# A fused two-model kernel: the last modulation steps moved behind the first direction of a recurrence in TensorE's order

## The chip, the cores and the metric

One Trainium2 chip, one of its cores. The metric is the device time of one execution in microseconds (us), lower is better. Engines: PE (TensorE), DVE (VectorE), ACT (ScalarE), POOL (GpSimd), SP (SyncE, which here only issues DMAs).

## What is computed

Two transformer blocks of two layers each run one after the other on 256 tokens of width 1024. The change lies in the last layer, whose mixer has a recurrence over the tokens (in two directions) beside a neighbourhood attention:

```python
def wkv7_step(S, inp):
    r, w, k, v, a, b = inp
    sa = jnp.einsum('bhvk,bhk->bhv', S, a)
    S = S * w[:, :, None, :] + sa[..., None] * b[:, :, None, :] + v[..., None] * k[:, :, None, :]
    return S, jnp.einsum('bhvk,bhk->bhv', S, r)
...
        mod = jnp.einsum('bd,de->be', jax.nn.silu(c), ada_w[i]) + ada_b[i]
        mod_c = jax.nn.silu(c_ctx) @ ada_w[i] + ada_b[i]
        sh1, sc1, g1, sh2, sc2, g2 = jnp.split(mod[:, None, :], 6, -1)
...
    x = x + g1 * y
    h = rms_norm_2(x, norm2_g[i]) * (1.0 + sc2) + sh2
    x = x + g2 * expert_choice_ffn(h, moe_router[i], moe_w1[i], moe_w3[i], moe_w2[i])
```

Each layer is modulated by six vectors (`sh1` to `g2`), a product of a 1024 vector with a 1024 x 6144 matrix. Behind the mixer stands a layer of 16 experts, whose weights are 192 MB.

## The kernel before, in words

All operations are written in program order, and a scheduler with a simulated timeline sets the order on each engine; within an engine the order is then fixed, and each engine and each DMA queue works through its own in that order. `later(offset, tag)` (line 300) adds to the priority number, so that a block with a large offset is put where the scheduler thinks that nothing earlier is ready.

*The recurrence* (`rwkv`, line 1897) is computed in chunks of 64 tokens. For each direction d and each of 4 blocks b of 128 channels: `decays` (1930) multiplies a triangular matrix `tri` with the gates on PE, in two halves of a block, each into a `py` bank of PSUM, takes exponentials on ACT (`win`, `AR`, `iin`, `Kh`) and forms the factors `Bh` and `Kh` on DVE and POOL. `within` (1983) forms products of these inside each chunk ("grams": `pg<-AR,Bh` on PE, masked by DVE into `Lx` and `Lc`). `spill` (1990) does the same with `Kh` (`MN`), multiplies with `V` (`py<-V,MN`), copies the result (`MV`, ACT) and transposes `Bh` and `Kh` on PE (`py<-cst,Bh`, `py<-cst,Kh`), which ACT copies (`zt`) and SP writes to DRAM (`sp<-MV`, `sp<-zt`). There are two `py` banks and two pairs of `pg` banks. With direction 0 the gates of direction 1 are prepared too (`begin(1)`, `low_rank`, line 1852).

Then each direction has a set of triangular systems: `gather` (2033) sends `Lx` and `Lc` through DRAM (`scr`) into another layout, `substitute` (2049) solves all systems of the direction at once by 31 steps of two DVE operations (`fs`, then `fsx` for direction 0 and `sgs` for direction 1), copies the result once and writes it to DRAM twice; `complete` (2067) reads it back (`kk`, `fsx`; `k`, `sgs`) and finishes the inverses on PE (`pg<-fsx,Lx` and so on; `pg<-sgs,Lx` is the first matmul of direction 1). DVE does the 62 operations of a direction between its work for `decays(1, b)`, `within(1, b)` and `spill(1, b)`. After that the chunks follow each other (the chain that begins with `pg<-mv,kk`), with the neighbourhood attention (`natten`, `pS<-nk,nq`, `pd<-low,nv`) between.

*The modulation* of this layer (`m`, `mods_steps`, line 508) is 3 banks of 8 steps; the first bank is done before the recurrence. A step is one slice of 128 rows: four loads of 128 x 512 (256 KB each, SP, `mod_weights`, 586) into the five `mw` tiles, and four matmuls, each into another 32 partitions of one `pd` bank. After the last step of a bank ACT copies it (`modrow`), PE transposes it (`pS<-cst,modrow`), DVE adds a bias (`modcol`), and the gates are transposed and written to DRAM (`gate_rows`, 545: `gatec`, `pS<-cst,gatec`, `modra`). `fill(n)` (2099) adds n steps at priority offset `OLATE`; `need(m, 2)` adds whatever is left. The `mw` tiles share their slots (tag `n2`) with the attention's `nbias` tiles.

Of the kernel before, what the change touches and what calls it, by code (L numbers as in the profile page):

```python
# [253 lines left out]
class Kernel:  # L254
# [75 lines left out]

    def mm(self, out, lhsT, rhs, start, stop):
        ins = self.nc.tensor.matmul(out, lhsT, rhs, start=start, stop=stop, skip_group_check=True)  # L332
        if self.pin:
            self.tc.keep_in_program_order(ins)
        return ins
# [1334 lines left out]

T2 = 16
SUB0, SUB1 = 0, 0
OLATE, OF = 2000, (2, 2, 2)
DECAY = math.exp(-0.5)


# [18 lines left out]
class Odd(Moe):  # L1695
# [201 lines left out]
    def rwkv(self, od, core, m):  # L1897
        nc, tc, a = self.nc, self.tc, self.a
# [15 lines left out]
        def begin(d):  # L1914
            S = st[d]

            S["AR"] = core.tile([128, 4, 768], F32, name=f"AR{d}")
            S["ARx"] = S["AR"][:, :, :512].rearrange("p b (i k t) -> p b i k t", k=4, t=64)
            S["sp"] = self.dram.tile([4, 128, 3, 512], F32, name=f"sp{d}")
            S["WC"] = core.tile([128, 4, 8], F32, name=f"WC{d}")  # L1920
            S["gr"] = core.tile([128, 2, 4, 2, 128], F32, name=f"Lx{d}")
            S["sgs"], S["av"] = self.rates[0] if d == 0 else self.low_rank(1, core, "t2", T2, "py")
# [60 lines left out]
        def within(d, b):  # L1983

            for th in range(2):
                p, mask = gram(st[d][b][0], d, b, th)
                L = st[d]["Lc"][:, :, b] if th else st[d]["gr"][:, :, b]
                nc.vector.tensor_tensor(L.rearrange("p t h c -> p h t c"), p, mask, OP.mult)
# [44 lines left out]
        def gather(d):  # L2033

            Lx, Lc = st[d]["gr"], st[d]["Lc"]
            scr = [self.dram.tile([4, 32, 32, 32], F32, name=f"scr{d}{i}") for i in range(3)]
            for q in range(4):
                hf, b2 = q // 2, q % 2
                ps_ = slice(64 * hf + 32 * b2, 64 * hf + 32 * b2 + 32)
                cs = slice(32 * b2, 32 * b2 + 32)  # L2040
                for i, gr in ((0, Lx[..., 64 * hf:64 * hf + 64]), (1, Lc)):
                    src = gr[ps_].rearrange("p t b h c -> p (t b h) c")[:, :, cs]
                    nc.sync.dma_start(scr[0][q, 16 * i:16 * i + 16].rearrange("u s t -> s u t"), src)
            LM = od.tile([128, 2, 32, 32], F32, name="sgs", bufs=1) if d else st[0]["LX"]
            LM, X = LM[:, 0], LM[:, 1]
            nc.sync.dma_start(LM, scr[0].rearrange("q u s t -> (q u) s t"))
            st[d].update(scr=scr, LM=LM, X=X)
# [51 lines left out]
        def fill(n):  # L2099
            with self.later(OLATE, "pS"):  # L2100
                self.fill(n)
# [3 lines left out]
        for b in range(4):  # L2105
            if b < 3:
                decays(0, b + 1)
            if b == 2:
                begin(1)
            within(0, b)  # L2110
            spill(0, b)
            fill(OF[0])
        gather(0)
        with self.later(SUB0, "pS"):
            substitute(0)
        for b in range(4):
            decays(1, b)
            within(1, b)
            fill(OF[1])
        gather(1)  # L2120
        with self.later(SUB1, "pS"):
            substitute(1)
        for b in range(4):
            spill(1, b)
            fill(OF[2])
        with self.later(OLATE, "pS"):
            self.need(m, 2)

        td = [p.tile([128, 4, 4, 2, 64], F32, name=n, bufs=1) for p, n in ((od, "kk"), (od, "k"))]
# [187 lines left out]
```

## Time and profile before

| | |
|---|---|
| median of 3 runs | 2812.18 us (2805.17 to 2812.28) |
| the profiled execution | 2812.01 us, span 2810.2 us |
| PE busy in the span | 2549.2 us (91%) |
| DVE, ACT, POOL busy | 1222.0, 773.3, 306.9 us |
| DMA | 683.94 MB, mean 243 GB/s |
| mean granted clock of PE | 0.957 |

The busy shares are averages over stages with different limits, so a stage is read by itself: its stretch of the span, who is busy in it, and which wait ends last. The granted clock is a share of full speed (2.4 GHz); PE has two levels, 1.2 and 2.4 GHz, and a share between stands for a stretch with both. In the trace a full-precision matmul has two rows. All times below are microseconds from the start of the span.

### The profile page before, as it was taken

To read this page: it belongs to the slowest core of one execution; us is meant where nothing else is said; L and a number is where in the kernel's file an instruction comes from. 1 tells how busy PE (TensorE), PEld (TensorE's weight loads), DVE (VectorE), ACT (ScalarE), POOL (GpSimd) and SP (SyncE) were. 2 spreads that over 40 slices of the span, in tenths; PEclk is the share of its full clock that TensorE was granted. 3 is DMA by queue.
4 is the path that set the end of the run, shared out by engine and by line. 5 is a ranking of instruction groups with operands and counts; after the bars stand their busy time and mean duration, and the time that the engine had idled before them with its cause. 6 is when DMAs were issued, how large, how long until landed. Compare 5 with 4: busy or idle time off the path is not lost.

```text
span 2810.2 us, 34392 instructions
## 1 busy us (share of the span) xinstructions
PE 2549.2 (91%) x13731; PEld 1567.7 (56%) x13731; DVE 1222.0 (43%) x2337; ACT 773.3 (28%) x1395; POOL 306.9 (11%) x372
## 2 busy tenths in 40 slices
PE   7999899996988998989899999989996997888888
PEld 4667688885866796757633333348644684222221
DVE  3355633448767467997511111145449452000000
ACT  3342322222333344276510000033442432000000
POOL 0001400004102003300100000000033130000000
PEclk9999999998989999999999999999998898999999
DMA  7443522233546854242699999963185548999998
GB/s 314 150 165 120 210 105 92 104 120 107 211 144 263 297 184 171 70 169 76 255 403 422 421 421 421 421 238 104 47 239 137 150 157 353 414 427 427 427 427 353
DMA packets 147360, 683.94 MB, mean 243 GB/s; under 512 B 38400, under 2 KB 51584, under 8 KB 72064
## 3 DMA queue, kind: packets, MB, share of 16 engines
q1 hardware_dynamic: 140656, 663.91, 61.2%
q10 hardware_dynamic: 6544, 17.83, 2.0%
q8 instruction: 108, 1.77, 0.3%
q14 instruction: 52, 0.43, 0.0%
HBM read 668.25 MB, written 11.60 MB: 242 GB/s over the span
## 4 chain that ended last, share of the span: by engine, by line
PE 52%; DMA 25%; DVE 8%; ACT 2%; issue 2%; POOL 1%; SPq 0%; ACTq 0%; DVEq 0%; POOLq 0%
DMA w<-in_moe_w 22%; PE pd L332 18%; PE pS L332 12%; PE pu L332 6%; PE pt L332 5%; PE ps L332 3%; PE pg L332 2%; PE pm L332 1%; DVE al L369 1%; PE pt L477 1%; PE ps L477 1%; DMA w<-in_od_w_in 1%; PE pO L332 1%; DVE fs L2060 1%; DVE co L1194 1%
## 5 line engine op out<-in xcount | busy, mean ns | idle before, releaser
L332 PE MATMUL pu<-w,xs 128*64 128x512 f32 (+1 forms) x2040 | 493.4, 599 | 40.9 <-DMA w<-in_moe_w 40.9
L352 ACT CAST wh<-w 128x1024 fp32r<-128x1024 f32 x250 | 259.5, 1041 | 602.9 <-PE pd L332 280.2
L355 DVE TENSOR_TENSOR wl<-w,wh 128x1024 fp32r<-128x1024 f32 x229 | 286.1, 1252 | 316.8 <-ACT wh L352 316.1
L332 PEld LDWEIGHTS pu<-w,xs 128*64 128x64 f32 (+1 forms) x2040 | 149.9, 123 | 367.1 <-issue 256.2
L332 PE MATMUL pd<-w,hidT 128*64 128x512 f32 (+1 forms) x1024 | 253.2, 598 | 28.8 <-DMA w<-in_moe_w 28.1
L332 PE MATMUL pd<-ah,wh 128*128 128x512 f32 (+2 forms) x656 | 232.9, 360 | 7.7 <-ACT wh L352 3.5
L332 PE MATMUL pd<-al,wh 128*128 128x512 f32 (+2 forms) x656 | 231.0, 354 | 7.5 <-DVE al L369 7.5
L332 PE MATMUL pd<-ah,wl 128*128 128x512 f32 (+1 forms) x648 | 226.3, 351 | 0.0
L1648 DVE TENSOR_TENSOR hid<-hid,pu 128x512 f32<-128x512 f32 x24 | 16.5, 688 | 434.4 <-PE pu L332 434.4
L1647 ACT ACTIVATE hid<-pu 128x512 f32<-128x512 f32 x24 | 14.2, 597 | 673.0 <-PE pu L332 673.0
L332 PEld LDWEIGHTS pd<-w,hidT 128*64 128x64 f32 (+1 forms) x1024 | 75.2, 123 | 197.3 <-issue 115.5
L332 PEld LDWEIGHTS pd<-ah,wh 128*128 128x128 f32 (+1 forms) x656 | 127.1, 195 | 40.2 <-issue 14.4
L332 PEld LDWEIGHTS pd<-al,wh 128*128 128x128 f32 (+1 forms) x656 | 128.0, 195 | 26.4 <-DVE al L369 8.9
L1657 DVE TENSOR_TENSOR ys<-pd,g 128x512 f32<-128x512 f32 x24 | 16.6, 692 | 282.4 <-PE pd L332 282.4
L332 PEld LDWEIGHTS pd<-ah,wl 128*128 128x128 f32 x648 | 126.2, 195 | 21.7 <-issue 7.5
L332 PE MATMUL pm<-w,sil 128*32 128x512 f32 x512 | 87.4, 711 | 30.8 <-DMA w<-in_ada_w 15.1
L1667 DVE TENSOR_TENSOR X<-X,ps 128x512 f32<-128x512 f32 x80 | 54.8, 688 | 109.2 <-PE ps L332 109.2
L1194 DVE SCALAR_TENSOR_TENSOR co<-cv,cols,co 128x512 f32<-128x512 f32 x120 | 100.6, 863 | 0.4
L332 PE MATMUL pS<-al,wh 128*128 128x256 f32 (+1 forms) x264 | 90.2, 342 | 5.5 <-DVE al L369 5.5
L332 PE MATMUL pS<-ah,wh 128*128 128x256 f32 (+1 forms) x264 | 90.1, 342 | 1.3 <-ACT ah L368 1.3
L332 PE MATMUL pS<-ah,wl 128*128 128x256 f32 (+1 forms) x264 | 89.3, 338 | 0.0
L354 POOL CAST hh<-tf 128x512 fp32r<-128x512 f32 (+1 forms) x64 | 37.3, 583 | 432.9 <-DVE tf L987 421.5
(601 smaller groups left out, 4527.2 us busy)
## 6 DMA issues: line engine op xcount, KB each, us to landing
w<-in_moe_w SPq DMA_DIRECT2D x383, 1024.0 KB, 19.6
w<-in_w_mod SPq DMA_DIRECT2D x32, 1024.0 KB, 6.0
w<-in_w_up SPq DMA_DIRECT2D x32, 1024.0 KB, 4.8
w<-in_w_down SPq DMA_DIRECT2D x32, 1024.0 KB, 4.8
w<-in_ada_w SPq DMA_DIRECT2D x32, 1024.0 KB, 5.0
w<-in_w_in SPq DMA_DIRECT2D x20, 1024.0 KB, 4.9
w<-in_modT SPq DMA_DIRECT2D x16, 1024.0 KB, 4.9
mw<-in_ada_w SPq DMA_DIRECT2D x64, 256.0 KB, 3.7
```

The source lines that it names most:

```text
L332: ins = self.nc.tensor.matmul(out, lhsT, rhs, start=start, stop=stop, skip_group_check=True)
L352: nc.scalar.copy(h, src)
L354: he.tensor_copy(h, src)
L355: (le or nc.vector).tensor_tensor(l, src, h.bitcast(F32), OP.subtract)
L369: nc.vector.tensor_tensor(l, t, h.bitcast(F32), OP.subtract)
L477: ins = self.nc.tensor.transpose(out, in_, self.ident[:rows, :rows])
L1194: nc.vector.scalar_tensor_tensor(y, CV[:, f, :, t:t + T], self.col(f"dw{t}", f), y, OP.mult, OP.add)
L1647: nc.scalar.activation(hid[:, cs], up["moe_w1_2"][c], AF.Silu)
L1648: nc.vector.tensor_tensor(hid[:, cs], hid[:, cs], up["moe_w3_2"][c], OP.mult)
L1657: nc.vector.tensor_tensor(ys[:, cs], down[c], gate[:, cs], OP.mult)
L1667: nc.vector.tensor_tensor(self.X[tb][:, cs], self.X[tb][:, cs], ps, OP.add)
L2060: nc.vector.tensor_tensor(t, LM[:, s, tr, None].to_broadcast([128, nt_, nj]), X[:, s, None, jr].to_broadcast([128, nt_, nj]), OP.mult)
```

## The change

Each matmul now leaves its instruction in `self.pe`. The fills behind `spill(0, b)` are gone. `held` is the last matmul of `spill(0, 3)`, and the modulation steps' PE instructions get an edge that puts them behind it in PE's order: two steps behind each `within(1, b)` and two behind each `spill(1, b)`. The edge is on PE alone; the loads on SP have none.

```diff
     def mm(self, out, lhsT, rhs, start, stop):
         ins = self.nc.tensor.matmul(out, lhsT, rhs, start=start, stop=stop, skip_group_check=True)
+        self.pe = ins
...
-OLATE, OF = 2000, (2, 2, 2)
+OLATE = 2000
...
             within(0, b)
             spill(0, b)
-            fill(OF[0])
+        held = self.pe
         gather(0)
         with self.later(SUB0, "pS"):
             substitute(0)
         for b in range(4):
             decays(1, b)
             within(1, b)
-            fill(OF[1])
+            with tc.issue_after(held.ins):
+                fill(2)
         gather(1)
         with self.later(SUB1, "pS"):
             substitute(1)
         for b in range(4):
             spill(1, b)
-            fill(OF[2])
-        with self.later(OLATE, "pS"):
+            with tc.issue_after(held.ins):
+                fill(2)
+        with self.later(OLATE, "pS"), tc.issue_after(held.ins):
             self.need(m, 2)
```

PE before, in the middle of the first direction (`pd<-mw,sil` are modulation matmuls):

```order
L332 MATMUL py<-V,MN 64x64 x16
L332 MATMUL pd<-mw,sil 32x512 x2
L332 MATMUL py<-V,MN 64x64 x8
L477 MATMUL py<-cst,Bh 128x128 x4
L332 MATMUL pd<-mw,sil 32x512
L332 MATMUL pg<-AR_13886,Bh 64x128 x8
L332 MATMUL pg<-AR_13886,Bh 64x64 x5
L477 MATMUL py<-cst,Kh 128x128 x4
```

The changed kernel has none there; 46 of the 64 stood in this direction before, the first now stands behind its last `py<-V,MN`.

PE of the changed kernel at the end of the second direction, from the last spilled block to the completion:

```order
L478 MATMUL py<-cst,Kh 128x128 x4
L332 MATMUL py<-V,MN 64x64 x24
L478 MATMUL py<-cst,Bh 128x128 x4
L332 MATMUL pd<-mw,sil 32x512
L478 MATMUL py<-cst,Kh 128x128 x4
L332 MATMUL pd<-mw,sil 32x512 x18
L478 MATMUL pS<-cst,modrow 128x128 x4
L478 MATMUL pS<-cst,gatec 16x128
L332 MATMUL pg<-fsx,Lx_13889 64x32 x32
```

Before, `pg<-fsx,Lx` followed the last `py<-cst,Kh` at once.

SP's queue of the changed kernel from the writing of the second direction's systems (`scr<-sgs`) to the attention's `nbias`:

```order
L592 DMA mw<-in_ada_w 128x512 x5
L2065 DMA scr_14874<-sgs 128x1024
L592 DMA mw<-in_ada_w 128x512
L2066 DMA scr_14875<-sgs 128x1024
L592 DMA mw<-in_ada_w 128x512 x4
L2080 DMA k<-scr_14875 32x32x32 x4
L2080 DMA sgs<-scr_14874 32x32x32 x4
L592 DMA mw<-in_ada_w 128x512 x3
L1884 DMA nbias<-in_na_bias 128x512 x4
```

Before, the two writes, the eight reads and three `nbias` loads followed each other with no `mw` load between. Ahead of this piece the changed queue has the four `sp<-zt` of the last block, and further up one run of 23 `mw` loads ahead of the second direction's gather.

## Rows read from the trace of the kernel before

**Rows 1.** Chain that ended last, a piece late in the span: start, us, what.
```profile
2443.60 19.57 DMA w<-in_moe_w
```
**Rows 2.** Timeline of SP's queue, its first expert loads: start, us, engine, line, operation.
```profile
2300.44 29.55 SPq L1628 DMA_DIRECT2D w<-in_moe_w  x15
```
**Rows 3.** Busy by stretch: PE, PEld, DVE, ACT, POOL (count); clock, DMA share, GB/s.
```profile
2033.90:2099.40 65.50, 64.17 (x591) 27.13 (x593) 30.04 (x51) 28.08 (x67) 20.48 (x22) 0.96 0.74 216
2099.40:2180.40 81.00, 52.60 (x744) 34.23 (x739) 75.33 (x181) 24.45 (x65) 28.36 (x24) 0.85 0.57 156
...
2180.40:2224.00 43.60, 37.27 (x466) 27.63 (x462) 17.42 (x37) 16.72 (x35) 1.80 (x1) 0.69 0.45 116
```
**Rows 4.** The same of the tile mw alone: PE, PEld, clock, DMA share, GB/s.
```profile
2033.90:2099.40 65.50, 32.95 (x92) 4.41 (x92) 0.96 0.74 216
2056.10:2067.60 11.50, 6.33 (x13) 0.83 (x12) 1.00 0.81 240
2099.40:2130.00 30.60, 12.94 (x36) 1.73 (x36) 0.94 0.65 201
```
**Rows 5.** Waits from 2033.9 to 2099.4: us in total, times, longest.
```profile
DVE Lx L1988 <- PE pg L332: 7.9, 3, 4.1
...
DVE Lc L1988 <- PE pg L332: 7.1, 3, 4.0
...
DVE MN L2001 <- PE pg L332: 5.1, 3, 2.9
```
**Rows 6.** Timeline of PE, ACT and DVE, one block of the first direction.
```profile
2056.12 0.38 PE L332 MATMUL py<-tri,sgs 128*128 128x256 f32 x1
...
2056.90 0.38 ACT L1947 ACTIVATE win<-py 128x256 f32<-128x256 f32 x1 [3.24 <-PE py L332]
...
2057.76 0.84 ACT L1959 ACTIVATE Kh<-av,ik,cols 128x512 f32<-128x512 f32 x1
...
2061.34 0.68 DVE L1958 TENSOR_TENSOR Bh<-Bh,iin 128x512 f32<-128x512 f32 x1
...
2063.84 0.68 PE L332 MATMUL py<-V,MN 64*64 64x64 f32 x16
...
2064.45 0.66 PE L477 MATMUL py<-cst,Bh 128*128 128x128 f32 x4
...
2067.66 0.39 PE L332 MATMUL py<-tri,sgs 128*128 128x256 f32 x1
```
**Rows 7.** The tile mw, its loads.
```profile
DMA to landing us min/median/max: 2.7/3.7/5.9
```
**Rows 8.** Timeline of PE, from the last spilled block to the chunk chain.
```profile
2173.70 1.06 PE L477 MATMUL py<-cst,Kh 128*128 128x128 f32 x4
...
2179.90 2.06 PE L332 MATMUL pg<-fsx,Lc 64*64 64x32 f32 x64
...
2193.42 3.62 PE L332 MATMUL pg<-sgs,Lx 64*64 64x32 f32 x62 [1.18 <-DMA sgs<-scr]
...
2224.06 0.97 PE L332 MATMUL pg<-mv,kk 64*64 64x64 f32 x13
```
**Rows 9.** Timeline of SP's queue, its issues.
```profile
2069.86 15.17 SPq L591 DMA_DIRECT2D mw<-in_ada_w  x13
...
2105.39 19.52 SPq L591 DMA_DIRECT2D mw<-in_ada_w  x13
...
2174.61 3.44 SPq L2031 DMA_DIRECT2D sp<-zt  x4
...
2180.39 0.34 SPq L2065 DMA_DIRECT2D scr<-sgs  x1
...
2187.50 3.52 SPq L2079 DMA_DIRECT2D sgs<-scr  x4
```
**Rows 10.** Timeline of ACT and PE behind a bank's last modulation matmul.
```profile
2129.72 0.58 ACT L531 COPY modrow<-pd 128x512 f32<-128x512 f32 x1 [6.74 <-PE pd L332]
...
2132.13 0.27 PE L477 MATMUL pS<-cst,gatec 128*16 128x128 f32 x1 [0.28 <-DVE gatec L551]
```

## The prediction

> **What bounds the kernel now.** I read the chain that ended last, then busy time by stretch, then the waits, then the timelines of PE and of SP's queue around the recurrence. The end of the kernel is a stream of expert weights: the chain hangs on one load after another [rows 1]. SP issues the first of those loads at 2300.44 us, after its last work for the recurrence [rows 2], and nothing behind it has slack. So what the recurrence gains or loses up to there is passed on microsecond for microsecond.
>
> The recurrence has three parts here. **First direction** (2033.9 to 2099.4, 65.5 us): PE is busy 64.17 us, DVE 30.04, ACT 28.08 [rows 3]; PE bounds it. Of PE's 64.17 us the modulation matmuls take 32.95 [rows 4]. **Triangular systems** (2099.4 to 2180.4, 81.0 us): DVE is busy 75.33, PE 52.60 [rows 3], of which 12.94 are modulation [rows 4]; DVE bounds it. **Completion and first attention heads** (2180.4 to 2224.0): PE 37.27 of 43.6 us at a granted clock of 0.69 [rows 3].
>
> **The change, part by part.** No operation is added or removed. There are 64 modulation matmuls (the trace has two rows for each), 46 in the first part and 18 in the second; each has its own load of 256 KB into one of five tiles. By the order none is left in the first part, 46 stand between the second part's matmuls, and 18 in one run behind the last of these, with the transposes that read them, ahead of the completion. The loads on SP's queue move along, but for the first five. Their small ACT, DVE and ACT-queue operations I cost at nothing until the last transposes: ACT is busy 24.45 of 81.0 us, and one bank's DVE work falls behind the systems.
>
> *First part: 17 us gained.* The bounds: nothing, if other engines were as late as PE; at most the time that DVE waited for PE here, 7.9 + 7.1 + 5.1 = 20.1 us [rows 5], since DVE's path starts the triangular system. Between them I walk one block in the new order, from its first `tri` half to the next block's; before, that took 2067.66 - 2056.12 = 11.54 us [rows 6]. Without modulation: a `tri` half until ACT reads it 0.8; win, AR and iin 0.9, Kh 0.8, the second half's three 0.9 (ACT); two multiplications and a mask at 0.6 (DVE); the V,MN group 0.6, the transposes of Bh and of Kh 0.6 each (PE); grams and hand-overs 1.2, my estimate. That is 8.2 us, with ACT and the two `py` banks late now instead of PE. The modulation taken out of the block is 6.33 us [rows 4]; 3.3 of them are gained, 0.53 of each microsecond. Of 32.95 us that is 17.4. I take 17: the part then lasts 48.5 us.
>
> *Second part: 2 us lost.* PE has 81.0 - 52.6 = 28.4 us free and gets some 11 us more modulation here (46 matmuls in about 24 groups of 1 us, 12.94 away). DVE's work is the same. But loads come at the pace of five tiles: 13 in a row took SP 15.17 and 19.52 us [rows 9], 1.2 to 1.5 us each, at 3.7 us to landing [rows 7]. 46 of them fit into 81 us, yet some grams of the second direction now stand behind a matmul that waits for its load, and DVE, in order, waits for the grams. Between 2 us less (the last bank's DVE work goes behind) and 7 more (a rival below) I take 2.
>
> *Behind it: 18 us lost.* Let u be the end of the last Kh transposes on PE, 2173.70 + 1.06 = 2174.8 before. There the completion began; it had both systems at 2193.42, u + 18.7, and the chunk chain began at 2224.06, u + 49.3 [rows 8]. Now 18 matmuls stand between. Four have their tiles. The fifth's load is issued at u; the next five loads stand on SP behind four issues of zt, which took 3.44 us [rows 9], so they are issued from u + 3 and used by u + 10. The five after those need these tiles, and stand around the writing of the second system, from 2180.39 (u + 5.6) on: used by u + 14. The last three stand behind the reading back of that system, whose issues ended at 2187.50 + 3.52 = 2191.0 [rows 9], u + 16.2, and end 2 us later with a load ahead of the second write: issue at u + 18.5, last matmul at u + 24. Row copy, transposes, DVE and gate transposes took from 2129.72 to 2132.40 [rows 10], so the completion starts at u + 27. From its start to the chunk chain it took 49.3 us with a wait for the second system; that is there now, and PE's own work is left, about 43 us at the clock it had, about 36 at the full one (the same 62 to 64 matmuls take 2.06 us fast and 3.62 slow [rows 8]). I take 40. The chunk chain starts at u + 67 against u + 49.3. The bounds are 8 us (the run over at u + 16, the rest fast) and 28 (all of the rest slow).
>
> Weighed against the rows: once it had waited for the second system, PE ran the completion slowly although it never idled, and the whole stretch was granted 0.69 [rows 3, 8], between the two levels of 1.2 and 2.4 GHz. My 40 us lean on that stretch. The Trainium skill (TensorE: Matmul & The Clock Gate, "HAM oscillation — how this bites in real kernels") says that short bursts of matmuls between waits for DMA keep falling back to the low clock; the run of 18 is such a stretch, and by that rule the sum would be that of the second rival.
>
> *Sum:* -17 + 2 + 18 = +3 us, against the profiled execution's 2812.0 us (span 2810.2), which lies 0.2 below the median of the runs: 2815 us. Three large terms nearly cancel; a measurement of this kernel can tell about 0.3%, 8.4 us, from no change.
>
> **The rivals.**
> *Faster: the run of 18 is short.* If its loads come as fast as tiles come free, it is over at u + 16 and the chunk chain starts 8 us late; if the first part gives up all 20.1 us, the sum is -20 + 0 + 8 = -12: 2800 us. For it: the DMA engines have room, a share of 0.45 behind 2180.4 [rows 3]. Against it: the queue order, with three loads behind the reading back.
> *Slower: the clock.* Packed with modulation the first part was granted 0.96; with 52.6 of 81.0 us busy the second was granted 0.85 [rows 3]. If PE, now with gaps, has 1.2 GHz for half of the first part, its shares of the walk grow and the gain is 12; if the completion is slow throughout, it takes 50 us instead of 40. Sum: -12 + 2 + 28 = +18: 2830 us. It decides from a granted clock below 0.8 in both stretches. The skill's rule named above is this rival.
> *Slower: DVE starved in the second part.* In one run SP's queue has the 23 loads that precede the second direction's gather. At 1.5 us each instead of 1.2 they end 7 us later, the second system starts late, and the sum is -17 + 2 + 7 + 18 = +10: 2822 us. Against it: DVE has the rest of the first system to do meanwhile.
> That the change does nothing can be left out: the order shows it.
>
> **How the numbers follow.** The forecast has 0.45; the faster rival 0.25; the clock 0.18; the starved DVE 0.12. Faster by over 0.3% is the first rival: 0.25. Slower is the two others: 0.30. Within: 0.45. The range goes from just below the faster rival to just above the clock's, 2798 to 2832; the forecast's own is 2806 to 2820, by the bounds nearest to each term.
>
> **What would show it.** First part: the first system starts near 2082 us instead of 2099.4, with no `mw` on PE and PE busy some 31 us. Second: from there to the last copy of the second system still 81 to 85 us. Behind: the completion's first matmul some 21 us after that copy, a run of `mw` ahead of it that waits for loads, then 40 us to the chunk chain. I am wrong if the first part gains under 12 us, if the run of 18 is over before the second system is read back, or if the second part grows by more than 6.

## The result and the profile after

The changed kernel took 2832.05 us (median of three runs, 2830.91 to 2834.74) against 2812.18: 19.9 us slower, ratio 1.0073 with an interval of 1.0051 to 1.0095. The forecast was 2815 us and no change. Its profiled execution took 2830.91 us, with a span of 2829.1.

Busy time by stretch in the changed kernel (columns as in [rows 3]): the first direction; from the first system to the end of the second; from the end of the last Kh transposes to the completion; from there to the chunk chain.

```profile
2033.10:2088.80 55.70, 41.39 (x472) 27.20 (x472) 27.46 (x46) 26.62 (x65) 20.79 (x22) 0.68 0.25 58
2088.80:2172.40 83.60, 63.84 (x673) 30.42 (x673) 75.04 (x179) 24.28 (x64) 27.84 (x24) 0.92 0.80 232
2167.20:2199.80 32.60, 20.02 (x43) 3.54 (x43) 5.33 (x20) 1.17 (x2) 1.80 (x1) 0.76 0.86 250
2199.80:2243.80 44.00, 44.00 (x609) 32.66 (x608) 17.63 (x37) 17.84 (x37) 0.00 (x0) 0.71 0.22 65
```

The first direction is 9.8 us shorter, but its clock fell from 0.96 to 0.68. The third stretch did not exist before; 18.59 of its 20.02 us on PE are modulation, against none at all in the first stretch. Its inside, in PE's timeline (start, us; in brackets the idle time before and what ended it):

```profile
2167.10 1.04 PE L332 MATMUL pd<-mw,sil 128*32 128x512 f32 x2
2168.54 2.34 PE L332 MATMUL pd<-mw,sil 128*32 128x512 f32 x6 [0.40 <-DMA mw<-in_ada_w]
2173.53 1.46 PE L332 MATMUL pd<-mw,sil 128*32 128x512 f32 x2 [2.65 <-DMA mw<-in_ada_w]
...
2192.83 4.20 PE L332 MATMUL pd<-mw,sil 128*32 128x512 f32 x6 [5.54 <-DMA mw<-in_ada_w]
2197.70 1.11 PE L478 MATMUL pS<-cst,modrow 128*128 128x128 f32 x4 [0.67 <-ACT modrow L532]
2199.49 0.37 PE L478 MATMUL pS<-cst,gatec 128*16 128x128 f32 x1 [0.67 <-DVE gatec L552]
2199.79 3.63 PE L332 MATMUL pg<-fsx,Lx 64*64 64x32 f32 x64
```

And on SP's queue, where before the reads were followed by `nbias`: the second write of the second system, its reading back, the last three loads, and the first expert load, which came at 2300.44 before [rows 2]:

```profile
2178.44 0.38 SPq L2066 DMA_DIRECT2D scr<-sgs  x1
...
2186.65 2.81 SPq L2080 DMA_DIRECT2D sgs<-scr  x4
2189.56 1.82 SPq L592 DMA_DIRECT2D mw<-in_ada_w  x3
...
2320.71 13.80 SPq L1629 DMA_DIRECT2D w<-in_moe_w  x7
```

The last three matmuls wait 5.54 us for loads issued behind the reading back of the second system. The expert stream starts 20.3 us later, and the span is 18.9 us longer: the difference arises ahead of that stream.

Stages in two profiles of each kernel, in us (starts and ends from PE's and DVE's timelines, rounded; u is the end of the last Kh transposes, as in the prediction):

| stage | before | again | after | again |
|---|---|---|---|---|
| first `tri` matmul to first system | 65.5 | 65.5 | 55.7 | 55.5 |
| to the end of the last Kh transposes (u) | 75.4 | 75.6 | 78.3 | 80.8 |
| u to the completion | 0 | 0 | 32.6 | 31.2 |
| completion to the chunk chain | 49.3 | 49.3 | 44.0 | 43.4 |
| sum | 190.2 | 190.4 | 210.7 | 210.8 |

### The profile page after: what moved, and what is told of

Its sections match the earlier page's. It is cut to its first block, busy times and chain, and to the rows that moved or that the text cites. A ratio compares the mean times of both kernels' runs of the same rounds, so it can differ in the third digit from the quotient of the medians.

```text
span 2829.1 us, 34407 instructions
## 1 busy us (share of the span) xinstructions
PE 2564.8 (91%) x13731; PEld 1572.6 (56%) x13731; DVE 1218.5 (43%) x2337; ACT 773.2 (27%) x1395; POOL 304.9 (11%) x372
## 4 chain that ended last, share of the span: by engine, by line
PE 51%; DMA 26%; DVE 7%; ACT 2%; issue 2%; POOL 1%; SPq 1%; ACTq 0%; DVEq 0%; POOLq 0%
DMA w<-in_moe_w 23%; PE pd L332 18%; PE pS L332 12%; PE pu L332 6%; PE pt L332 5%; PE ps L332 3%; PE pg L332 3%; PE pm L332 1%; DVE al L370 1%; PE pt L478 1%; DMA mw<-in_ada_w 1%; PE ps L478 1%; DMA w<-in_od_w_in 1%; PE pO L332 1%; PE py L332 1%
## 5 line engine op out<-in xcount | busy, mean ns | idle before, releaser
L332 PE MATMUL pm<-w,sil 128*32 128x512 f32 x512 | 87.1, 715 | 29.0 <-DMA w<-in_w_mod 14.1
L1668 DVE TENSOR_TENSOR X<-X,ps 128x512 f32<-128x512 f32 x80 | 54.8, 687 | 113.3 <-PE ps L332 113.3
L332 PE MATMUL ps<-ys,gt 128*128 128x512 f32 x160 | 82.7, 627 | 2.1 <-DVE X L1668 2.1
```

What stands on the lines that cost most here:

```text
L1668: nc.vector.tensor_tensor(self.X[tb][:, cs], self.X[tb][:, cs], ps, OP.add)
```

## The experiments

Unless told otherwise, edits are made to the changed kernel. "Chain" is the start of the chunk chain, counted from the first `tri` matmul: 190.2 before, 210.7 after. Ratios are to the kernel before, run beside each of them.

**Second profiles** (no edit).

> The changed kernel once more, for a second profile. If the tail's term is the run and its loads: the run from the last Kh transposes to the completion again 28 to 34 us, first part 55 to 57 us, time 2826 to 2836 us. If the first profile was an unlucky one (the completion's clock differs from profile to profile of one kernel, as the kernel with the masks first showed: 32.6 and 43.7 us): run below 26 us or completion below 36 us, time below 2824 us.

> The kernel before once more, for a second profile: the stages of the first one hold if the first part is 65 to 66 us, the second 80 to 83, and the chunk chain comes 187 to 194 us behind the first tri matmul.

The changed kernel took 2832.21 us, ratio 1.0092 (1.0075 to 1.0109); the kernel before took 2815.83 us in its one run. In the table above each stage came again within 2.5 us, so the terms belong to the kernels and not to one execution.

**Nearly no modulation**, in the changed order (e_none) and in the order before (e_noneb):

```
-            for k in range(KT):
+            kn = 1 if self.modpool else KT
+            for k in range(kn):
...
-                            k == 0, k == KT - 1)
-                if k < KT - 1:
+                            k == 0, k == kn - 1)
+                if k < kn - 1:
```

> The changed kernel with one step instead of eight in each of the two modulation banks of the recurrence: 14 of 16 steps, 56 of the 64 loads and matmuls, are left out. What stays is the order of the change with nothing to hide and next to nothing in the run at the end. Clock theory (PE without modulation falls to 1.2 GHz in the first part, and the run at the end is the tail's cost): first part again 54 to 57 us, clock again below 0.75; the last Kh transposes within 3 us of the changed kernel; from there to the chunk chain 43 to 50 us instead of 76.6; time 2832 - 30 = about 2802 us. Rival (the first part was slowed by the loads and tiles of the modulation, which the change only moved): first part 48 to 50 us and time 2794 us. Rival (the tail is slow for the clock alone, run or no run): from the last transposes to the chunk chain 60 us or more, 2818 us.

> The kernel before the change with one step instead of eight in each of the two modulation banks (56 of 64 loads and matmuls left out), in its own order: the 8 that stay are in the first part. It shows what the modulation cost before the change, the most that any hiding can give back. If the first part's floor is 55.7 us whatever the order (clock and low-rank chain): first part 55 to 59 us, and the time is 2802 to 2808 us, as with the changed order. If the changed order has a disadvantage of its own: 2797 us or less.

Changed order: 2805.17 us, ratio 0.9985 (0.9972 to 0.9997), chain 185.3. First part and tail came as expected (55.7 us; u to the chain 44.7), but u came 84.9 us after the first system instead of 78.3, 6.5 us later, outside the expected 3. Order before: 2814.01 us, ratio 1.0012 (0.9995 to 1.0029), chain 192.2, slower than expected. First directions of e_none and of e_noneb, and the completion of e_noneb:

```profile
2034.90:2090.60 55.70, 41.46 (x472) 27.27 (x472) 27.44 (x46) 26.62 (x65) 20.77 (x22) 0.68 0.24 57
```
```profile
2034.00:2088.80 54.80, 45.32 (x498) 26.70 (x498) 29.50 (x55) 28.22 (x69) 20.52 (x22) 0.78 0.31 80
...
2172.20:2226.20 54.00, 54.00 (x610) 38.99 (x609) 17.80 (x37) 18.52 (x37) 1.32 (x1) 0.56 0.36 88
```

So about 55 us is what the first direction takes with next to no modulation, in either order; the loads that the change moved have no part in it. And taking 56 of 64 matmuls out of the kernel before saves nothing that can be measured: what the first direction gains (10.7 us) goes into a second part 83.4 us long up to u (75.4 before) and a completion at a clock of 0.56, 54.0 us instead of 49.3. Why u comes later in both, these runs leave open. Before the change the modulation was as good as free; there was little to win.

**The tail alone** (e_tail): 12 of 16 steps free to go into the first direction, four held ahead of the completion.

```
             spill(0, b)
-        held = self.pe
+            fill(2)
...
-            with tc.issue_after(held.ins):
-                fill(2)
+            if b < 2:
+                fill(2)
...
             spill(1, b)
-            with tc.issue_after(held.ins):
-                fill(2)
+        held = self.pe
```

> The tail alone: 12 of the 16 steps may go into the first direction as before the change (the order puts 48 matmuls there), and only the last 16 matmuls are held behind the second direction's last spilled block, ahead of the completion. Theory (the run costs what its loads take, and the first part's gain is another matter): first part 64 to 67 us as before at a clock above 0.9, from the last Kh transposes to the chunk chain 20 to 27 us more than the 49.3 before, time 2812 + 20 to 27 = 2832 to 2839 us. Only 5 + 11 matmuls wait there and the tiles are free early, so the lower end is likelier. Rival (the tail cost came from the moved first part, which makes loads stand late everywhere): under 10 us more, time below 2822 us.

2826.66 us, ratio 1.0068 (1.0041 to 1.0095). First part 65.0 at a clock of 0.96; u to the completion 17.5, u to the chain 59.4, chain 204.3. The tail costs 10 us more than before, not 20 to 27, and u itself comes 4.5 us later (79.8 us after the first system, 75.4 before). The run of 16 is about half as long as that of 18 in the changed kernel; its last five loads were issued at u + 6.6, ahead of the reading back, where the changed kernel's last three came at u + 22.4, behind it. The direction was right, the size was not; the rival's 10 us were missed by little, its time by 5 us.

**A fourth back in the first direction** (e_mid1).

```
             spill(0, b)
-        held = self.pe
+            held = self.pe
+            fill(1)
```

> A fourth of the modulation back in the first direction: one step behind each of its four blocks (16 matmuls there by the order), the 48 others held as in the change and all but 5 of them between the second part's matmuls. Theory (clock and run): the first part is granted more than 0.8 and takes 54 to 58 us, no longer than without any modulation; the run at the end is gone, from the last Kh transposes to the chunk chain 45 to 52 us; time 2800 to 2808 us. Rival (PE's work sets the first part): it grows by 16 x 0.72 = 11.5 us to 67 us and all of the change's gain is gone, 2812 to 2816 us. Rival (the loads, not the order, set the end): the run is gone but the last loads still come late, the tail stays above 65 us, 2825 us.

2823.19 us, ratio 1.0056 (1.0040 to 1.0073): a miss. First part (58.1 us, at a clock of 0.79) and run (3.2) came close to what was expected, but the second part grew to 93.7 us and the completion had a clock of 0.58. SP's queue shows a part of the cause, the run of loads ahead of the second gather (25.44 us for the same 23 in the changed kernel):

```profile
2110.76 31.54 SPq L592 DMA_DIRECT2D mw<-in_ada_w  x23
2142.34 0.42 SPq L2044 DMA_DIRECT2D scr<-Lx  x1
```

The gather starts 46.7 us after the first system instead of 42.2, and later DVE waits 4.1 us (0.9 in the changed kernel) before the column add of a bank (`modcol`), whose transposes are late on PE. This looks like my rival of the starved DVE, in another kernel than the one it was written for; no run took these waits away to test it.

**Idle matmuls for the clock**: 16 in the blocks (e_warm), or 4 in the low-rank part (e_warmL).

```
+        idle = self.psum("pd")
+
+        def warm(n, pe):
+            with self.later(OLATE, "pS"), tc.issue_after(pe.ins):
+                for _ in range(n):
+                    nc.tensor.matmul(idle[:32], self.ident[:, :32], self.tri, start=True, stop=True, skip_group_check=True)
+
+        warm(4, self.pe)
...
-        held = self.pe
+            held = self.pe
+            if b < 3:
+                warm(4, held)
```

(This is e_warm; e_warmL has the same loop without `later`, called with 2 from `low_rank` in its first two steps of direction 1.)

> The changed kernel with 16 idle matmuls of the modulation's shape in the first part, on tiles that lie in SBUF, into the bank that is free there: 4 ahead of the first block and 4 behind each of the first three. They compute nothing that is used and load nothing. Clock theory: the first part is granted more than 0.85, its low-rank matmuls take 2.1 us for two instead of 3.78, and though PE has some 11 us more to do the part gets shorter, 50 to 54 us instead of 55.7; time 2826 to 2830 us. Rival (the first part hangs on ACT and DVE, not on PE's clock): it stays at 55 to 57 us whatever the clock. Rival (PE's work sets it): 60 us or more, 2837 us.

> The changed kernel with 4 idle matmuls of the modulation's shape, nothing computed with them and nothing loaded: two behind each of the first two low-rank matmuls of the second direction, where the changed kernel's PE waits 0.4 and 1.6 us before it goes on at 1.2 GHz. Clock theory: the six low-rank matmuls behind them stay at 1.0 to 1.1 us for two records instead of 1.9, the stretch from the first low-rank matmul to the mask of the last block (17.5 us in the changed kernel) takes 12 to 14 us, and the first part 51 to 53 us instead of 55.7. Rival (ACT and DVE set this stretch): clock high, but the first part still 55 us or more. Rival (the clock falls there anyway): granted clock below 0.7 from the low-rank matmuls on, first part 56 to 58 us.

e_warm: 2846.51 us, ratio 1.0149 (1.0130 to 1.0169). Its first part, halved at the first low-rank matmul, and the same of the changed kernel:

```profile
2036.80:2070.40 33.60, 28.47 (x354) 18.02 (x353) 18.21 (x31) 14.79 (x46) 15.15 (x16) 0.85 0.21 55
2070.40:2091.80 21.40, 19.41 (x145) 9.24 (x144) 9.00 (x16) 10.37 (x18) 5.08 (x7) 0.84 0.30 65
```
```profile
2033.10:2061.40 28.30, 21.35 (x337) 17.45 (x337) 17.07 (x29) 14.24 (x43) 14.67 (x15) 0.74 0.18 48
2061.40:2088.80 27.40, 20.03 (x137) 9.76 (x136) 10.39 (x18) 12.39 (x23) 6.11 (x8) 0.62 0.32 68
```

The low-rank half is 6.0 us shorter at 0.84, the other 5.3 longer by the idle work: 55.0 us in all. How much of the 6.0 is the clock, and how much ACT and DVE catching up in the longer half, this run cannot say. e_warmL (2834.01 us, ratio 1.0093, 1.0071 to 1.0115): the low-rank matmuls next to the idle ones stayed fast (1.12 us for two records), the clock fell on the four behind them after two waits of 1.4 and 1.5 us, and the first part took 57.6 us. In neither did idle work on PE make the first part clearly shorter. In both, the second part was longer too, 89.5 and 90.9 us; why, these runs leave open.

**The run cut short** (e_short), the rest as in e_none:

```
-            for k in range(KT):
+            kn = 4 if self.modpool and bank == 2 else KT
+            for k in range(kn):
```

> The changed kernel with four of the eight steps of the last modulation bank left out (16 of 64 loads and matmuls; that bank's result is then a sum over half of its rows): the order leaves 3 or 4 matmuls behind the second part instead of 18. Theory (the run is the tail's cost): first part 55 to 57 us as in the changed kernel, from the last Kh transposes to the chunk chain 46 to 54 us instead of 76.6, time 2804 to 2811 us. Rival (the 46 matmuls among the second part's own starve DVE and only the shift of the bottleneck hid it): the second part grows to 88 us or more and the time stays above 2818 us.

2809.12 us, ratio 1.0001 (0.9987 to 1.0015). First part 55.7, u to the completion 3.9, u to the chain 53.4: with the run the tail's cost goes, and the chain (190.0) is where it was before the change. The rival had a point too: the second part took 90.2 us, with a wait of DVE that stands between the steps of the second system:

```profile
DVE modcol L541 <- PE pS L478: 4.6, 1, 4.6
```

**Loads of the last five steps on ACT's queue** (e_queue).

```
...
-                self.nc.sync.dma_start(wt, src[:, g * 512:(g + 1) * 512])
+                eng.dma_start(wt, src[:, g * 512:(g + 1) * 512])
...
```

(`eng` is `nc.scalar` for `bank == 2 and k > 2`, else `nc.sync`.)

> The changed kernel with the loads of the last five modulation steps (20 of 64 loads) issued from ACT's queue instead of SP's, where three of them stood behind the reading back of the second system. PE's order keeps a run of 17. If the queue's order sets the length of the run (my step for the tail): the longest wait of the run, 5.5 us, goes, the run from the last Kh transposes to the completion takes 20 to 24 us instead of 32.6, and the time is 2820 to 2824 us. Rival (the DMA engines set it: their share was 0.86 in the run): it stays at 28 us or more, 2828 to 2834 us. Rival (ACT, held up by issues that wait for tiles, copies late): the second system ends later by 5 us or more, 2836 us.

2818.95 us, ratio 1.0046 (1.0023 to 1.0068). The run: 22.1 us, its longest wait 2.5; u to the chain 54.7 instead of 76.7. The second system ended 91.0 us after the first began (83.6 in the changed kernel), so ACT's issues seem to have cost something. The DMA engines did not set the length of the run: their share was 1.02 in it, against 0.86, and it was shorter. But these 22 us are not all the queue's. Of them 11.4 are the completion, which had the full clock in this profile (32.6 us instead of 44.0). The run gives the other 10.6, and u itself came 6.0 us later, so from the first system the completion began only 4.6 us earlier (106.4 us instead of 111.0).

**The first system behind the last mask** (e_mn, and again as e_mn2).

```
-                nc.vector.tensor_tensor(MN, p, mask, OP.mult)
+                self.mn = nc.vector.tensor_tensor(MN, p, mask, OP.mult)
...
         gather(0)
-        with self.later(SUB0, "pS"):
+        with self.later(SUB0, "pS"), tc.issue_after(self.mn.ins):
             substitute(0)
```

> The changed kernel with the first direction's triangular system ordered behind that direction's last mask on DVE. In the changed kernel the last mask stood behind eight steps of the system, so the last spilled block, and with it the first modulation matmul that is held behind it, came at 2096 us, 7.5 us after the system had begun. Theory (the whole stream of loads starts with it and ends as much earlier): first modulation matmul 3 us or less after the system's first step, the run at the end shorter by 5 to 9 us (23 to 27 instead of 32.6), time 2823 to 2827 us. Rival (PE order and tiles set it, not the start): run unchanged within 2 us, 2830 to 2833 us.

> The same kernel as the one with only the first direction's system behind the last mask on DVE, once more. In its first profile the chunk chain stood 185.5 us behind the first tri matmul, 4.6 less than before the change, and the first expert load at 2299.5 us; but the expert loads then moved 387 and 400 GB/s for 200 us where all other profiles show 427, and the time was 2821.5 us. If that was a disturbance of that run: 427 GB/s there, time 2803 to 2815 us. If the kernel causes it: again below 405 GB/s, 2819 us or more.

2821.51 us, ratio 1.0042 (1.0022 to 1.0062), then 2817.30, 1.0016 (0.9998 to 1.0034). The first modulation matmul came before the system's first step (2089.83 against 2093.42; in the changed kernel it came 7.5 us after that step), the first part stayed at 55.8 us, and the run took 26.3 and 27.2 us, as the theory had it. From the first system the completion began 97.1 and 97.9 us later, instead of 111.0. The two profiles differ in the completion, and with it in the chain (185.5 and 197.4):

```profile
2190.50:2223.20 32.70, 32.70 (x610) 24.41 (x609) 17.50 (x37) 17.53 (x37) 0.00 (x0) 1.00 0.45 121
```
```profile
2189.70:2233.40 43.70, 43.40 (x610) 31.82 (x609) 17.62 (x37) 17.95 (x37) 0.00 (x0) 0.73 0.35 92
```

The same 610 records take 32.7 us at the full clock and 43.7 at 0.73. The question put to e_mn2 has a mixed answer: the expert loads were fast again (420 and 427 GB/s), but the time stayed above the 2803 to 2815 us that were expected for that.

**Idle matmuls in the gap of the run** (e_gap), behind its 15th matmul:

```
+                    if self.modpool and bank == 2 and k == 7 and g == 1:
+                        idle, ins = self.psum("py"), self.pe
+                        for _ in range(6):
+                            with self.tc.issue_after(ins.ins):
+                                ins = nc.tensor.matmul(idle[:32], sl[:, k, :], self.V[:, 0], start=True, stop=True,
+                                                       skip_group_check=True)
...
```

> The changed kernel with 6 idle matmuls of the modulation's shape on tiles that lie in SBUF, between the 15th and the 16th matmul of the run at the end, where PE waited 5.5 us for the last three loads. Loads, their order and everything else are as in the change. Clock theory (that wait takes PE to 1.2 GHz and the completion pays for it): the wait in the run is under 2 us, the completion is granted 0.9 or more and takes 33 to 37 us to the chunk chain instead of 44.0, the run is no longer than 34 us, time 2820 to 2826 us. Rival (the completion is slow by itself, by its small matmuls and the waits for ACT and DVE): granted 0.7 as before, 43 to 45 us, time 2831 to 2835 us.

2828.50 us, ratio 1.0055 (1.0035 to 1.0075): the theory fell. The 5.5 us wait was filled and the completion began fast, but not for long:

```profile
2189.12 5.31 PE L531 MATMUL py<-V,sil 128*32 128x512 f32 x12
2195.27 2.40 PE L332 MATMUL pd<-mw,sil 128*32 128x512 f32 x6 [0.84 <-DMA mw<-in_ada_w]
2198.35 0.66 PE L478 MATMUL pS<-cst,modrow 128*128 128x128 f32 x4 [0.68 <-ACT modrow L543]
2199.67 0.27 PE L478 MATMUL pS<-cst,gatec 128*16 128x128 f32 x1 [0.67 <-DVE gatec L563]
2199.87 2.06 PE L332 MATMUL pg<-fsx,Lx 64*64 64x32 f32 x64
2201.86 3.50 PE L332 MATMUL pS<-nk,nq 64*128 64x512 f32 x4
```

The first group took 2.06 us instead of 3.63, then the clock fell after all, and the completion took 47.9 us at 0.64. In the 25 us ahead of it PE had not waited longer than 0.89 us at a time, so a long wait just ahead of the completion is not needed for a slow one. What made the clock fall here, the run does not show.

**Two attempts at a better kernel**, both with e_mn's edit: two steps back in the first direction (e_half, the diff), or the second bank's loads on ACT's queue (e_best2, as e_queue but for all `k`).

```
             spill(0, b)
-        held = self.pe
+            held = self.pe
+            if b < 2:
+                fill(1)
```

> Two changes to the changed kernel: the first direction's system is ordered behind that direction's last mask on DVE, and one modulation step stands unheld behind each of the first two blocks of the first direction (8 matmuls there by the order); 5 matmuls are left in the run at the end. Theory (first part at its floor, run short, completion at full clock): first part 55 to 58 us, second part 82 to 86, chunk chain 176 to 184 us behind the first tri matmul where the kernel before took 190.2 and the changed one 210.7: time 2798 to 2808 us. Rival (the floor that the kernel without most modulation showed, 2805, is all there is, and each load that PE waits for in the second part delays DVE): 2808 to 2818 us.

> The changed kernel with the first direction's system behind the last mask on DVE and all loads of the second of the two modulation banks (32 of 64) issued from ACT's queue; a run of 8 matmuls is left at the end. Theory: first part 56 us, run 10 to 16 us, completion 33 us, chunk chain 178 to 186 us behind the first tri matmul, time 2800 to 2810 us. Rival (ACT's issues wait for tiles and hold its copies, so that DVE waits in the second part): second part 90 us or more, time 2815 to 2825 us.

2819.19 us, ratio 1.0024 (1.0010 to 1.0037), and 2816.81, 1.0018 (0.9996 to 1.0041): both theories missed. In e_half the first part took 53.9 us, but the second 93.7, and the completion 54.0 at a clock of 0.56 (chain 202.3); in e_best2 the run took 13.7, but the second system ended only 86.7 us after the first began and the completion took 44.6 at 0.71 (chain 197.1). Neither beats the kernel before.

## Why the prediction was wrong

The chain came 20.5 us later instead of 3: 9.8 gained in the first direction, 2.9 lost up to u, 27.4 lost behind it. Two terms were mis-sized, the gain by 7 us and the tail by 9; the prediction's own sign of being wrong, a gain under 12 us, came true.

**First direction: forecast 17 us gained, measured 9.8.** The step that failed is "Of 32.95 us that is 17.4", one block's ratio spread over the whole part. The walk itself was good: the block took 8.8 us from `tri` to `tri` (2050.66 to 2059.44), 8.2 were forecast. The tile `mw` in the kernel before, halved at the first low-rank matmul (columns as in [rows 4]):

```profile
2033.90:2072.10 38.20, 19.71 (x54) 2.58 (x54) 0.94 0.69 206
2072.10:2099.40 27.30, 13.24 (x38) 1.83 (x38) 1.00 0.81 230
```

Ahead of the low-rank matmuls the part went from 38.2 to 28.3 us, with 19.71 us of modulation gone: half of each microsecond, as in the block. From the low-rank matmuls on it went from 27.3 to 27.4, with 13.24 gone: nothing. There PE's own work grew from 14.1 us (27.3 less 13.24, at full clock) to 20.0 at 0.62 (the halves beside e_warm's), and the rest became waits for ACT, DVE and the gather. The runs with next to no modulation put the whole part at 54.8 and 55.7 us, far above the forecast's 48.5.

How much of this the clock did can be read closer, in two rows of the changed kernel and in e_noneb's halves, cut at the same place:

```profile
2069.67 3.78 PE L332 MATMUL py<-lwa,low 64*128 64x512 f32 x4 [0.22 <-DVE sg L1866]
...
2078.91 0.42 DVE L1989 TENSOR_TENSOR Lc<-pg,cst 128x256 f32<-128x256 f32 x1 [3.65 <-PE pg L332]
```
```profile
2034.00:2062.00 28.00, 25.12 (x363) 16.82 (x363) 19.13 (x37) 15.85 (x47) 14.43 (x15) 0.92 0.31 88
2062.00:2088.80 26.80, 20.21 (x137) 9.88 (x136) 10.37 (x19) 12.37 (x23) 6.09 (x8) 0.64 0.32 70
```

Ahead of the low-rank matmuls the clock made no difference that shows: e_noneb took 28.0 us at 0.92, with its eight modulation matmuls, and the changed kernel 28.3 at 0.74. In the other half it stood on the path. From 2065.67 to the last `Lc` mask PE waited 0.22 us in all, and the mask waited for PE; the six low-rank matmuls there took 11.3 us, at a granted clock of 0.50, where the two ahead of them took 1.12 each. That is 4.6 us more; e_warm's half, at 0.84, was 6.0 shorter. From the end of that mask to the first system it took 9.5 us before and after.

**Second part: forecast 2 lost, measured 2.6** (83.6 against 81.0; 2.9 up to u). Right, but by little margin: kernels with almost the same order showed 90.2 (e_short) and 93.7 (e_mid1).

**Tail: forecast 18 lost, measured 27.4** (u to the chain 76.7 against 49.3). Two sizes were off. The run ended at u + 29.9, not u + 24: the second write of the second system, with six loads ahead of it on SP's queue, was issued at u + 11.3, where it came at u + 5.6 before, and with it the three last loads came at u + 22.4 instead of u + 18.5; the last matmuls took 4.20 us at the low clock. And the completion took 44.0 us, not 40. That the run is the tail's cost holds (e_short, which leaves most of it out, has the chain where it was before). That the place of the last three loads in SP's queue sets its length holds only in part (e_queue). I priced queue places, and put the late start of the stream at nothing. From its first matmul to its last the 64 took 100.7 and 102.3 us in the two profiles of the changed kernel, 98.5 and 99.3 in e_mn's and 96.7 in e_queue, 1.5 to 1.6 us for each load; and it began 7.5 us after the first system. In e_mn, counted from the first system, its first matmul came 11.1 us earlier and its last 13.3 us.

**The rival that came about is the clock**: 0.68 and 0.71, both below the 0.8 from which it decides, with a gain of 9.8 where it said 12 and a time of 2830 where 2832 was measured. That the times agree is partly luck: its 28 us of tail were a completion of 50 us, and the 27.4 came from a longer run and a completion of 44.0. The rule of the Trainium skill that I named beside it (TensorE: Matmul & The Clock Gate, "HAM oscillation — how this bites in real kernels") agrees with the trace in the run of bursts between waits: it was granted 0.76, and the six records behind the wait of 5.54 us took 4.20 us, where the six at 2168.54 took 2.34. The completion behind it was granted 0.50 for its first 20 us, though PE was busy throughout. But such a run does not settle a case alone: those of e_queue and e_mn are of the same kind, and their completions had the full clock. I gave the rival 0.18 although [rows 3] already showed 0.85 and 0.69 where PE has gaps, and my own change opened gaps in the part that had 0.96. Part of its price was already in the kernel before, though: the completion then had 0.72 (0.62 in the second profile).

**The faster rival** needed the run over at u + 16 and all 20.1 us of the first part. Even with next to no modulation the changed order was only 0.15% faster (e_none).

**What held**, to about 4 us, is that nothing behind the recurrence has slack: from the chunk chain to the end of the span it took 582 to 586 us in all profiles but two, the first of e_mn and that of e_best2, which took 600 and 599 (the last section has what differed there).

## What to carry to other kernels

Filler work that is taken out of a stretch leaves gaps. Here the granted clock fell with it, and PE's own work grew from 14.1 to 20.0 us: before costing a move, ask what the stretch would take with the filler left out altogether, and run that kernel first. Price a ratio from one block only where the block repeats. And work that is pushed back with its loads is paid where its last load lands: add the start of the stream to the number of loads at their pace, and compare that with the end of the work which was to hide them.

## What the runs showed of the hardware

The clock of one and the same stretch of one kernel differs between executions: the completion was granted 1.00 and 0.73 in two profiles of e_mn (32.7 and 43.7 us). Over the kernels in which PE hardly waits in it the pairs line up: 1.00 with 32.7, 0.76 with 41.9, 0.71 with 44.0 and 44.6, 0.62 with 49.8, 0.56 with 54.0. So such a stretch can by itself set two executions of one kernel 11 us apart; in the two profiles of the changed kernel it did not (44.0 and 43.4). And the first profile of e_mn, like that of e_best2, moved only 387 and 400 GB/s (385 and 397) for 200 us of the expert stream, where e_mn2 had 420 and 427; what disturbed it, no run shows.
